# A hybrid decoder layer on one core: the first scaling and the sums of the output product stand in another order, six remainders of the mLSTM values are made by accumulating transfers, and the gates' first row waits for a sum

## The chip, the core and the metric

The kernel runs on one core of a Trainium2 chip. The metric is the device time of one execution in microseconds; the times shown are three executions of the kernel before, and one more execution was profiled. The engines are named as in the profile: PE (matrix products), DVE (vector), ACT (scalar), POOL (GpSimd) and SP (which only issues transfers here).

## What is computed

One layer of a decoder on 512 tokens with 1024 channels, in float32. The parts that the change touches:

```python
h = rmsnorm(x, norm_mix_g)                     # first scaling
proj = h @ w_in                                # mLSTM q, k, v, output gate; attention q, k, v; gates
lf = log_sigmoid(gates[..., ML_HEADS:])        # the gates' rows: lf, its sums, the running maximum
h_ml = mlstm_chunkwise(q_ml, k_ml, v_ml, ig, lf)
...
merged = sigmoid(g_a) * (y_a @ w_branch_a) + sigmoid(g_b) * (y_b @ w_branch_b)
x = x + merged @ w_out                         # output product
x = x + square(relu(rmsnorm(x, norm_mlp_g) @ w_up)) @ w_down
x = x + sigmoid(rmsnorm(x, norm_ple_g) @ w_ple_gate) * (p @ w_ple_proj)
return rmsnorm(x, final_norm_g)
```

## The kernel before

**Products in two parts.** Every float32 operand of a product is split into a high part (a rounding copy) and a low part (the remainder `value - high`), and three products high·high, high·low, low·high are summed in PSUM (`pairs`, `chain`). The high part of a weight is mostly an ACT cast (`wh`, L137), the low part a DVE subtraction (`wl`, L138). `split_by_transfer` (L144 to L148) makes the remainder in another way: ACT writes the high part (L146), ACT writes the negated value into the low tile (L147), and a transfer that POOL issues adds the value to it in memory (L148).

**Stages around the change.** The program first multiplies the per-layer embedding `p` by its weight (`early`: high parts `eh` on ACT and POOL at L303 and L305, remainders on DVE at L306), norms the four token tiles of `x` (`norm`: ACT squares and a root, DVE reciprocal and scaling, L341), turns them by PE transposes (`columns`, L354) and splits the result into `h` (ACT L359, DVE L360). The early products' PSUM is copied out (`pe`, L385 to L394) before the attention values (`vs`) take its bank. Then come the attention keys and the first queries, the mLSTM values (`w_vml`), the output gate (`w_o`), the branch gates (`w_gb`, `w_ga`), attention mixed with the other projections, mLSTM, the merge, the output product and the MLP.

**Seven products instead of eight.** `seven` computes a product of two-by-two blocks with seven block products in PSUM groups X, Y, Z. After the first block product (p1, `A11`) ACT copies X out (L570), and the second (`A12`) adds to X, so PE waits for that copy. t21 and t22 are sums that DVE makes from Z (L573); c11, c22, c12, c21 are the results. `by_tokens` runs it for `w_vml` and then for `w_o`; the sums and differences of weight blocks are DVE operations of 128x1024 (L510, L511, L520, L524). For the values, `put_v` adds the kept part on DVE (L597), casts the high part on ACT (L598), subtracts on DVE for the low part (L599) and stores the low part to memory by a POOL transfer (L584). The output product (`out_proj`, from L1108) does the same by hand: its first product is F11, then ACT copies X to `q1` (L1144), and F12 adds to X; `b11 + b12` is L1151, `b21 - b11` is L1160, `b22 - b11` is L1161.

**What sets the order.** A scheduler sorts the instructions of each engine when the program is built, by its own estimate of when each is ready; each engine then works its list strictly in order. `tc.issue_after(x)` lays an edge: the instructions in its block on x's engine come behind x. Tiles come from pools with a fixed number of buffers: weights `wr` 4, `wh` 4, `wl` 4, scratch `lm` 4, activations `act` 34. A transfer into a buffer waits until its last reader is done.

Of the kernel before, what the change touches and what calls it, by code (L numbers as in the profile page):

```python
# [13 lines left out]
ALU = mybir.AluOpType  # L14
# [22 lines left out]
def block_kernel(  # L37
# [30 lines left out]
    V, A, G, T = nc.vector, nc.scalar, nc.gpsimd, nc.tensor  # L68
# [43 lines left out]
    def act_hl(n="s"):  # L112
        return [act_r(n), act_r(n)]
# [15 lines left out]
    def r32(t):  # L129
        return t.bitcast(F32)  # L130
# [13 lines left out]
    def split_by_transfer(dst, src):  # L144

        A.copy(dst[0], src)  # L146
        A.activation(dst[1], src, AF.Copy, scale=-1.0)  # L147
        return nc.gpsimd.dma_start(out=r32(dst[1]), in_=src, accum_op=ALU.add)  # L148
# [146 lines left out]
    spare = ps_a()  # L295
    early_ps = [spare[:, :512], spare[:, 512:], ps_g(), ps_g()]

    def early_part(k):
        parts = []
        for i, t in enumerate(early[k]):  # L300
            hl = act_hl("eh")
            if k or i:
                G.tensor_copy(hl[0], t)  # L303
            else:
                p_high = A.copy(hl[0], t)  # L305
            V.tensor_sub(hl[1], t, r32(hl[0]))  # L306
            parts.append(hl)
        return parts, p_high if k == 0 else None

    def early_products(k, parts):  # L310
        for m in range(NT):
            chain(early_ps[m], pairs([q[:, m * P : (m + 1) * P] for q in parts[0]], parts[1]), k == 0, k == 1, True)

    e0, p_high = early_part(0)
    e1, _ = early_part(1)
    early_products(0, e0)

    rooted = [None]
# [48 lines left out]
    def load_vs_w(c):  # L367
        n = K3[c].stop - K3[c].start
        hl = [wp.tile([P, 1024], F32R, tag=t, bufs=WB, name=nm(t))[:, : n * 264] for t in ("wh", "wl")]
        w_high = G.tensor_copy(hl[0], wv[c][:, : n * 264])  # L370
        last_low[0] = V.tensor_sub(hl[1], wv[c][:, : n * 264], r32(hl[0]))
        return [q.rearrange("p (k c) -> p k c", k=n) for q in hl]

    with tc.issue_after(p_high.ins):
        xn, normed = norm(0)
    with tc.issue_after(normed):
        wv[0] = load_vs_w(0)
    xn1, normed = norm(1)
    with tc.issue_after(normed):
# [15 lines left out]
    on_scalar, on_vector = columns(1, xn1)  # L395
    for m in range(NT):
        if m == 1:
            columns(2, xn2)
        elif m == 2:
            with tc.issue_after(on_scalar):  # L400
                xn, _ = norm(3)
            _, on_vector = columns(3, xn)

        ps = ps_g()
        for c in range(3):
            mm_tok(ps[:, :264], wv[c], hT[K3[c]], m, first=c == 0, last=c == 2)
        t = sp.tile([P, 256], F32, tag="vs", bufs=4, name=nm("vs"))
        A.copy(t, ps[:, :256])
        gate_in = V.tensor_add(gt[:, m, :], ps[:, 256:264], bif)
        vs.append(t)  # L410
# [3 lines left out]
        mm_T(ps, load_w(wd[i], KT * P, KT), hT)  # L414
        return ps

    with tc.issue_after(on_vector):
        wk0 = load_w(w_ksw[0], KT * P, KT)

    hf[0] = tk("hf")[:, :D].rearrange("p (k c) -> p k c", k=KT)  # L420
# [141 lines left out]
    def post_by_tokens(done):  # L562

        keep = {}

        def post(what, ps):
            for t in range(2):
                if what == "p1":
                    keep["p1", t] = act_f("p1")
                    A.copy(keep["p1", t], ps[t])  # L570
                elif what[0] == "t":
                    keep[what, t] = act_f(what)
                    V.tensor_add(keep[what, t], ps[t], keep["p1", t])  # L573
                else:
                    k = None if what == "c11" else keep["p1" if what == "c12" else "t" + what[1:], t]
                    done(t + (2 if what[1] == "1" else 0), int(what[2]) - 1, ps[t], k)

        return post

    kept = []  # L580

    def store_low():
        for o, t in kept:
            nc.gpsimd.dma_start(out=o, in_=t)  # L584
        kept.clear()

    def put_v(m, nh, ps, k):
        if k is not None:
            store_low()
        o = vm[m][:, 2 * nh : 2 * nh + 2, :DV]  # L590
        two = lambda t: t.rearrange("p (h d) -> p h d", h=2)
        low = act_r("vl")
        if k is None:
            A.copy(o, two(ps))
            V.tensor_sub(two(low), two(ps), r32(o))
        else:
            V.tensor_add(k, ps, k)  # L597
            A.copy(o, two(k))  # L598
            V.tensor_sub(two(low), two(k), r32(o))  # L599
        kept.append((vld[:, 2 * nh : 2 * nh + 2, m, :], two(r32(low))))  # L600

    pg = ps_a()
# [3 lines left out]
        T.transpose(pgf[:4, m * P : (m + 1) * P], gt[:, m, 4:], ident)  # L606
    by_tokens(w_vml, post_by_tokens(put_v), True)
    store_low()


    def row(n):
        return c1.tile([P, 512], F32, tag="row", bufs=NH, name=nm(n))
# [25 lines left out]
    def gates():  # L638

        lf = row("lf")[:4, :]  # L640
        V.scalar_tensor_tensor(lf, fg, -1.0, fg, ALU.mult, ALU.max)
        A.activation(lf, lf, AF.Exp, scale=-1.0)
        A.activation(lf, lf, AF.Ln, bias=1.0)
        V.scalar_tensor_tensor(lf, fg, 0.0, lf, ALU.min, ALU.subtract)
        mst = act_f("mst")[:4, :]
        V.tensor_tensor_scan(mst, lf, ig, 0.0, ALU.add, ALU.max)
        fl = row("fl")[:4, :]
        for c in range(NT):
            V.tensor_tensor_scan(fl[:, c * P : (c + 1) * P], lf[:, c * P : (c + 1) * P], zeros4, 0.0, ALU.add, ALU.add)
# [415 lines left out]
    for j in range(4):  # L1065
        m0 = merge(2 * j)
        if j == 0:
            load_out(1)
            load_out(3)
        elif j < 3:  # L1070
            b = b_out[1][j - 1]
            V.tensor_sub(b, b_out[3][j - 1], b)
        else:
            for m in range(NT):
                nc.sync.dma_start(out=xk[m], in_=x[m * P : (m + 1) * P, :])
        later = merge_sums(m0, merge(2 * j + 1))
        if j < 3:
            later()

# [33 lines left out]
    def out_proj():  # L1113

        b11, b12, b21, b22 = b_out
        X = [ps_g(), ps_g()]
        Y, Z = [[t[:, 0, :], t[:, 1, :]] for t in (pair(), pair())]

        def form(raw):
            return load_w(None, 1024, 2, raw)  # L1120

        def half(ps, f, w, kh, first, last):
            for t in range(2):
                ops = []
                for k in range(2):
                    ops += pairs([h[:, t * P : (t + 1) * P] for h in f[2 * kh + k]], [h[:, k, :] for h in w])
                chain(ps[t], ops, first and kh == 0, last and kh == 1, True)

        def prod(ps, f, b, first, last):
            for kh in range(2):  # L1130
                half(ps, f, form(b[kh]), kh, first, last)

        def part_of(r, c, t):
            return xk[t + (2 if r == 1 else 0)][:, (c - 1) * 512 : c * 512]

        def acc(ps, r, c):
            for t in range(2):
                o = part_of(r, c, t)
                V.tensor_add(o, ps[t], o)

        prod(X, F11, b11, True, False)
        q1 = [act_f("q1") for _ in range(2)]
        for t in range(2):
            copied = A.copy(q1[t], X[t])  # L1144
        with tc.issue_after(copied.ins):
            later()
        for r, c in ((2, 1), (2, 2), (1, 2)):
            for t in range(2):
                nc.gpsimd.dma_start(out=part_of(r, c, t), in_=q1[t], accum_op=ALU.add)
        for kh in range(2):  # L1150
            V.tensor_add(b11[kh], b12[kh], b11[kh])  # L1151
        prod(X, F12, b21, False, True)
        acc(X, 1, 1)
        with tc.issue_after(last_mm[0].ins):
            prod(Z, G2, b11, True, False)
        acc(Z, 2, 1)
# [12 lines left out]
        half(Z, G4, form(b22[1]), 1, False, True)  # L1169
        acc(Z, 1, 2)  # L1170
# [386 lines left out]
```

## Time and profile before

| what | value |
|---|---|
| three runs | 877.5, 878.6, 879.84 us (median 878.6) |
| profiled execution, its own time | 877.63 us |
| its span, first to last instruction | 875.5 us |
| mean granted PE clock | 0.999 |
| busy PE / DVE / ACT / POOL | 862.2 / 674.4 / 488.9 / 51.4 us |

The profiled execution's own time is 2.1 us above its span; the rest lies before the first and behind the last instruction. Times in the rows below count from the start of the span. A row of the timeline gives start, duration, engine, line, operation, tiles, shape and count, and in brackets the idle time of the engine before it with what ended it. A duration of PE is that of a pipelined matmul; the distance of two starts is what one costs. The same holds on DVE and ACT, where the next operation starts about 0.08 us before the one ahead of it ends.

### The profile page before, as it was taken

The page shows a single profiled execution, that of the slowest core. Times are in us where ns is not written, and L with a number is a line of the kernel's source. Part 1 is how long each engine was busy: PE and PEld are TensorE (multiplying, and loading weights), DVE is VectorE, ACT ScalarE, POOL GpSimd, SP SyncE. Part 2 cuts the span into 40 slices and gives each one's busy share as a digit, 9 for nine tenths or more (in the row PEclk, how much of TensorE's full clock was granted, in tenths as well). Part 3 has the DMA queues.
Part 4 walks back from the last instruction along what each step waited for, and adds up shares of the span by engine and source line. Part 5 has one row for each costly group of instructions (what it writes and reads, how often), then busy time and mean ns, then how long its engine had stood idle before and what let it go on. Part 6 is the DMA issues. An engine that isn't in the chain of part 4 may idle for free.

```text
span 875.5 us, 11759 instructions
## 1 busy us (share of the span) xinstructions
PE 862.2 (98%) x4422; PEld 725.2 (83%) x4422; DVE 674.4 (77%) x998; ACT 488.9 (56%) x825; POOL 51.4 (6%) x81
## 2 busy tenths in 40 slices
PE   9999999999999999999999999999999999999996
PEld 7878789999877778888878888888888888888886
DVE  7899979785688898867897668756975795678657
ACT  6785556444586667853343566345535633564743
POOL 3221111000000000000020000000000000002000
PEclk9999999999999999999999999999999999999999
DMA  8686236445121255665334710531162044206502
GB/s 285 212 204 254 107 109 204 146 144 197 69 73 49 96 185 194 211 252 183 107 53 137 249 66 25 205 119 38 62 224 100 1 142 171 73 24 133 180 1 97
DMA packets 36234, 117.76 MB, mean 135 GB/s; under 512 B 5069, under 2 KB 5069, under 8 KB 36178
## 3 DMA queue, kind: packets, MB, share of 16 engines
q1 hardware_dynamic: 28578, 95.77, 31.2%
q0 software_dynamic: 7456, 20.98, 8.8%
q8 instruction: 35, 0.57, 0.3%
q10 hardware_dynamic: 144, 0.26, 0.1%
q14 instruction: 21, 0.17, 0.1%
HBM read 99.17 MB, written 11.54 MB: 126 GB/s over the span
## 4 chain that ended last, share of the span: by engine, by line
PE 87%; DVE 6%; ACT 3%; DMA 2%; issue 2%; SPq 0%; ACTq 0%; DVEq 0%
PE psg L176 48%; PE psp L176 23%; PE psa L176 6%; PE pst L176 2%; PE pst L836 2%; DVE wl L138 1%; PE psp L1105 1%; DMA wq<-in_w_o 1%; PE psa L778 1%; DMA xt<-in_x 1%; PE psa L779 1%; ACT wh L137 1%; PE psa L918 1%; PE psa L940 1%; PE psa L938 1%
## 5 line engine op out<-in xcount | busy, mean ns | idle before, releaser
L137 ACT CAST wh<-wr 128x1024 fp32r<-128x1024 f32 x129 | 135.6, 1053 | 156.4 <-PE psg L176 62.7
L138 DVE TENSOR_TENSOR wl<-wr,wh 128x1024 fp32r<-128x1024 f32 x129 | 156.8, 1219 | 74.2 <-ACT wh L137 73.1
L176 PE MATMUL psg<-x,wh 128*128 128x512 f32 x512 | 157.8, 389 | 0.0
L176 PE MATMUL psp<-wh,uf 128*128 128x512 f32 x448 | 138.6, 389 | 0.0
L176 PEld LDWEIGHTS psg<-x,wh 128*128 128x128 f32 x512 | 96.1, 188 | 19.9
L176 PE MATMUL psg<-x,wl 128*128 128x512 f32 x256 | 99.6, 389 | 0.0
L176 PEld LDWEIGHTS psp<-wh,uf 128*128 128x128 f32 x448 | 84.1, 188 | 17.5
L176 PE MATMUL psp<-wl,uf 128*128 128x512 f32 x224 | 87.2, 389 | 0.0
L176 PE MATMUL psg<-h,wh 128*128 128x512 f32 x256 | 80.9, 395 | 0.7 <-DVE rc L804 0.7
L137 ACT CAST wh<-wd 128x1024 fp32r<-128x1024 f32 x44 | 46.2, 1053 | 54.3 <-PE psp L176 21.9
L138 DVE TENSOR_TENSOR wl<-wd,wh 128x1024 fp32r<-128x1024 f32 x44 | 53.1, 1218 | 14.7 <-ACT wh L137 14.5
L176 PEld LDWEIGHTS psg<-x,wl 128*128 128x128 f32 x256 | 48.1, 188 | 9.9
L176 PEld LDWEIGHTS psg<-h,wh 128*128 128x128 f32 x256 | 46.9, 188 | 11.2 <-issue 1.6
L176 PE MATMUL psg<-h,wl 128*128 128x512 f32 x128 | 50.5, 395 | 0.0
L138 DVE TENSOR_TENSOR uf<-F,uf 128x1792 fp32r<-128x1792 f32 (+2 forms) x20 | 33.0, 1652 | 21.8 <-ACT uf L137 21.8
L176 PEld LDWEIGHTS psp<-wl,uf 128*128 128x128 f32 x224 | 42.1, 188 | 8.7
L176 PE MATMUL psg<-yb,wh 128*128 128x512 f32 x128 | 40.4, 393 | 0.0
L1273 DVE SCALAR_TENSOR_TENSOR xk<-psp,r,xk 128x512 f32<-128x512 f32 x48 | 33.8, 745 | 8.0 <-PE psp L176 7.7
L176 PE MATMUL psg<-ya,wh 128*128 128x512 f32 x128 | 39.8, 391 | 0.0
L137 ACT CAST uf<-F 128x1792 fp32r<-128x1792 f32 (+2 forms) x20 | 27.9, 1396 | 20.5 <-DVE F L1249 20.4
L176 PE MATMUL psa<-h,wh 128*128 128x256 f32 x192 | 35.5, 285 | 0.6 <-ACT p L714 0.5
L176 PE MATMUL psg<-hS,wh 128*128 128x256 f32 x192 | 35.7, 285 | 0.2 <-DVE t L704 0.2
(356 smaller groups left out, 1836.1 us busy)
## 6 DMA issues: line engine op xcount, KB each, us to landing
wr<-in_w_up SPq DMA_DIRECT2D x32, 512.0 KB, 3.2
wd<-in_w_down SPq DMA_DIRECT2D x24, 512.0 KB, 3.8
wr<-in_w_qsw SPq DMA_DIRECT2D x8, 512.0 KB, 4.3
gd<-gr POOLq DMA_DIRECT2D x8, 512.0 KB, 3.1
wr<-in_w_qkml SPq DMA_DIRECT2D x8, 512.0 KB, 3.2
wr<-in_w_b SPq DMA_DIRECT2D x8, 512.0 KB, 3.2
wh<-in_w_b POOLq DMA_DIRECT2D x8, 512.0 KB, 3.8
gl<-gd SPq DMA_DIRECT2D x8, 512.0 KB, 3.3
```

Of the source, the lines that this page charges most:

```text
L137: A.copy(dst[0], src)
L138: last_low[0] = V.tensor_sub(dst[1], src, r32(dst[0]))
L176: last_mm[0] = T.matmul(ps, l, r, start=first and i == 0, stop=last and i == len(ops) - 1, skip_group_check=parts)
L778: T.matmul(o, q[:, n * P : (n + 1) * P], kk[kp][ab][:, k0 : k0 + 256], start=True, stop=False)
L779: T.matmul(o, q[:, n * P : (n + 1) * P], kl[kp][ab][:, k0 : k0 + 256], start=False, stop=True)
L836: T.matmul(o[HALF[ab], :], v[:, c : c + 64], w[:, ab * 512 : (ab + 1) * 512], start=j == 0, stop=j == len(terms) - 1)
L918: T.matmul(psc[s], l, r, start=j == 0, stop=j == 2, skip_group_check=True)
L938: T.matmul(o, hi, vm[s][:, h, :], start=s == 0, stop=False, skip_group_check=True)
L940: last_mm[0] = T.matmul(o, lo, vm[s][:, h, :], start=False, stop=s == t, skip_group_check=True)
L1105: T.transpose(ps[:, c, m * P : (m + 1) * P], xk[m][:, (k + c) * P : (k + c + 1) * P], ident)
L1273: V.scalar_tensor_tensor(o, ps[:, t, :], r2[:, 2 * toks + t : 2 * toks + t + 1], o, ALU.mult, ALU.add)
```

## The change

Four edits. First, the early remainders are made in two separate steps: those of the first half stand where they stood, those of the second half (`early_low(1, e1)`) behind the first scaling; the norm of the last token tile moves ahead of `columns(2)`, and `columns(2)` behind it. Second, the three values results that need a sum (c22, c12, c21, two tiles each) get their low part by `split_by_transfer` in place of the DVE subtraction, and their stores lag by two. Third, the gates' first row operation (DVE) is laid behind the last t22 sum that is recorded in `summed`. Fourth, `b11 + b12` of the output product is laid behind the remainder of the last merge.

```diff
-    def early_part(k):
-        parts = []
-        for i, t in enumerate(early[k]):
-            hl = act_hl("eh")
-            if k or i:
-                G.tensor_copy(hl[0], t)
-            else:
-                p_high = A.copy(hl[0], t)
-            V.tensor_sub(hl[1], t, r32(hl[0]))
-            parts.append(hl)
-        return parts, p_high if k == 0 else None
+    def early_high(k):
+        parts = [act_hl("eh"), act_hl("eh")]
+        for hl, t in zip(parts, early[k]):
+            done = (G.tensor_copy if k or hl is parts[1] else A.copy)(hl[0], t)
...
+    def early_low(k, parts):
+        for hl, t in zip(parts, early[k]):
             V.tensor_sub(hl[1], t, r32(hl[0]))
...
-    e0, p_high = early_part(0)
-    e1, _ = early_part(1)
+    e0, p_high = early_high(0)
+    e1, _ = early_high(1)
+    early_low(0, e0)
     early_products(0, e0)
...
     with tc.issue_after(normed):
+        early_low(1, e1)
         wv[0] = load_vs_w(0)
...
         if m == 1:
-            columns(2, xn2)
+            with tc.issue_after(on_scalar):
+                xn, normed = norm(3)
+            with tc.issue_after(normed):
+                turned_third, _ = columns(2, xn2)
         elif m == 2:
-            with tc.issue_after(on_scalar):
-                xn, _ = norm(3)
             _, on_vector = columns(3, xn)
...
-                    V.tensor_add(keep[what, t], ps[t], keep["p1", t])
+                    summed[0] = V.tensor_add(keep[what, t], ps[t], keep["p1", t])
...
-    def store_low():
-        for o, t in kept:
+    def store_low(last=0):
+        while len(kept) > last:
+            o, t = kept.pop(0)
             nc.gpsimd.dma_start(out=o, in_=t)
-        kept.clear()
...
-            store_low()
+            store_low(2)
...
             V.tensor_add(k, ps, k)
-            A.copy(o, two(k))
-            V.tensor_sub(two(low), two(k), r32(o))
+            split_by_transfer([o, two(low)], two(k))
...
+    values_sum = summed[0]
...
-        V.scalar_tensor_tensor(lf, fg, -1.0, fg, ALU.mult, ALU.max)
+        with tc.issue_after(values_sum.ins):
+            V.scalar_tensor_tensor(lf, fg, -1.0, fg, ALU.mult, ALU.max)
...
-        later = merge_sums(m0, merge(2 * j + 1))
+        m1 = merge(2 * j + 1)
+        merged = last_low[0]
+        later = merge_sums(m0, m1)
...
-        for kh in range(2):
-            V.tensor_add(b11[kh], b12[kh], b11[kh])
+        with tc.issue_after(merged.ins):
+            for kh in range(2):
+                V.tensor_add(b11[kh], b12[kh], b11[kh])
```

Because the scheduler sorts anew, more moves than the diff shows. Three places follow. Lines of the changed kernel lie up to six higher.

**DVE at the start.** `eh_28`/`eh_30` and their partners are the early remainders of the second half, `xn_33` the first token tile, `wl_38` the low part of the first piece of the attention values' weight. Before:

```order
L306 TENSOR_TENSOR eh_28_177<-p_7_111,eh_27_176 128x512
L306 TENSOR_TENSOR eh_30_181<-wp_8_112,eh_29_180 128x512
L326 RECIPROCAL rs_36_204<-sd_35_202 128x1
L341 SCALAR_TENSOR_TENSOR xn_33_199<-xt_1_102,rs_36_204,psa_15_146 128x512 x2
L326 RECIPROCAL rs_42_217<-sd_41_215 128x1
L371 TENSOR_TENSOR wl_38_209<-wr_10_122,wh_37_208 128x792
```

And now:

```order
L327 RECIPROCAL rs_36_202<-sd_35_200 128x1
L342 SCALAR_TENSOR_TENSOR xn_33_197<-xt_1_102,rs_36_202,psa_15_146 128x512 x2
L308 TENSOR_TENSOR eh_28_175<-p_7_111,eh_27_174 128x512
L308 TENSOR_TENSOR eh_30_177<-wp_8_112,eh_29_176 128x512
L372 TENSOR_TENSOR wl_38_209<-wr_10_122,wh_37_208 128x792
L327 RECIPROCAL rs_42_217<-sd_41_215 128x1
```

The first scaling passed the two remainders, which now stand directly ahead of `wl_38`.

**DVE from the values' second half into the output gate's product.** `wq_182`/`wq_183` are sums of `w_o` blocks, `wl_173`/`wl_175` the low parts of the values' last product, `t22`, `p1`, `t21` the values' results c22, c12, c21, `wl_200` the low part that the output gate's second product reads. Before:

```order
L138 TENSOR_TENSOR wl_173_895<-wr_117_616,wh_172_894 128x1024
L510 TENSOR_TENSOR wq_182_946<-wq_186_954,wq_182_946 128x1024
L597 TENSOR_TENSOR t22_158_805<-psa_121_624,t22_158_805 128x512
L597 TENSOR_TENSOR t22_159_807<-psa_121_624,t22_159_807 128x512
L138 TENSOR_TENSOR wl_175_911<-wr_118_618,wh_174_910 128x1024
L599 TENSOR_TENSOR vl_164_843<-t22_158_805,vm_108_590 128x512
L599 TENSOR_TENSOR vl_165_848<-t22_159_807,vm_109_592 128x512
L597 TENSOR_TENSOR p1_130_661<-psg_124_627,p1_130_661 128x512
L138 TENSOR_TENSOR wl_194_964<-wr_180_942,wh_193_963 128x1024
```

And now, from the sum on:

```order
L513 TENSOR_TENSOR wq_182_952<-wq_186_960,wq_182_952 128x1024
L600 TENSOR_TENSOR t22_158_805<-psa_121_624,t22_158_805 128x512
L600 TENSOR_TENSOR t22_159_807<-psa_121_624,t22_159_807 128x512
L138 TENSOR_TENSOR wl_173_897<-wr_117_616,wh_172_896 128x1024
L138 TENSOR_TENSOR wl_175_913<-wr_118_618,wh_174_912 128x1024
L513 TENSOR_TENSOR wq_183_954<-wq_187_962,wq_183_954 128x1024
L600 TENSOR_TENSOR p1_130_661<-psg_124_627,p1_130_661 128x512
L138 TENSOR_TENSOR wl_194_970<-wr_180_948,wh_193_969 128x1024
L600 TENSOR_TENSOR p1_131_663<-psg_125_628,p1_131_663 128x512
L138 TENSOR_TENSOR wl_196_986<-wr_181_950,wh_195_985 128x1024
L514 TENSOR_TENSOR wr_180_948<-wq_182_952,wr_180_948 128x1024
L514 TENSOR_TENSOR wr_181_950<-wq_183_954,wr_181_950 128x1024
```

The remainders (L599) are gone, but `wl_173` now stands behind the sum, and the second sums stand further ahead. The next three rows are `wl_200` and the two sums of c21; before, `wl_200` stood behind c21 and its remainders.

**ACT at the first product of `w_o`, and at the output product.** `wh_205` is a cast for the third product, `p1_197` the copy of X. Before, and now:

```order
L598 CAST vm_108_590<-t21_152_769 128x2x256
L598 CAST vm_109_592<-t21_153_771 128x2x256
L137 CAST wh_205_1042<-wr_180_942 128x1024
L570 COPY p1_197_995<-pst_189_959 128x512
L570 COPY p1_198_997<-pst_190_960 128x512
```

```order
L146 CAST vm_108_590<-t21_152_769 128x2x256
L147 ACTIVATE vl_176_929<-t21_152_769 128x512
L146 CAST vm_109_592<-t21_153_771 128x2x256
L147 ACTIVATE vl_177_935<-t21_153_771 128x512
L137 CAST wh_205_1048<-wr_180_948 128x1024
L573 COPY p1_197_1001<-pst_189_965 128x512
L573 COPY p1_198_1003<-pst_190_966 128x512
```

Two more passes stand ahead of the copy. In the output product the cast `wh_853` of `b11` after its sum stands ahead of the copy of X, `q1_845`, in both; but its sum (L1157 now) has moved on DVE behind the last merge:

```order
L137 CAST mg_825_4593<-sga_824_4590 128x512
L137 CAST ms_829_4603<-ms_827_4597 128x512
L137 CAST wh_853_4707<-wr_831_4607 128x1024
L1149 COPY q1_845_4657<-psg_837_4621 128x512
L1149 COPY q1_846_4658<-psg_838_4622 128x512
```

What moved there is the moment at which the cast's input is ready.

More of the change, by code (lines that the diff above doesn't have):

```diff
@@ L296, in block_kernel @@
     early_ps = [spare[:, :512], spare[:, 512:], ps_g(), ps_g()]
-    def early_part(k):
-        parts = []
-        for i, t in enumerate(early[k]):
-            hl = act_hl("eh")
-            if k or i:
-                G.tensor_copy(hl[0], t)
-            else:
-                p_high = A.copy(hl[0], t)
+    def early_high(k):
+        parts = [act_hl("eh"), act_hl("eh")]
+        for hl, t in zip(parts, early[k]):
+            done = (G.tensor_copy if k or hl is parts[1] else A.copy)(hl[0], t)
+            if not k and hl is parts[0]:
+                first = done
+        return parts, first if k == 0 else None
+    def early_low(k, parts):
+        for hl, t in zip(parts, early[k]):
             V.tensor_sub(hl[1], t, r32(hl[0]))
-            parts.append(hl)
-        return parts, p_high if k == 0 else None
     def early_products(k, parts):
@@ L415, in proj_T @@
         return ps
-    with tc.issue_after(on_vector):
+    with tc.issue_after(on_vector), tc.issue_after(turned_third):
         wk0 = load_w(w_ksw[0], KT * P, KT)
```

## The prediction

> **What bounds the kernel now.** I read the page first.
>
> ```profile
> span 875.5 us, 11759 instructions
> PE 862.2 (98%) x4422; PEld 725.2 (83%) x4422; DVE 674.4 (77%) x998; ACT 488.9 (56%) x825; POOL 51.4 (6%) x81
> PE 87%; DVE 6%; ACT 3%; DMA 2%; issue 2%; SPq 0%; ACTq 0%; DVEq 0%
> ```
>
> PE is busy for 862.2 of 875.5 us and makes 87% of the chain that ended last. The change takes no matmul away and adds none. So it acts only through moments at which PE stands still, and each of its four edits must be costed at the PE wait beside it. The list of PE's waits came second.
>
> ```profile
> PE pst L176 <- DVE wl L138: 0.9, 1, 0.9
> PE psg L176 <- DVE sga L1020: 0.9, 1, 0.9
> PE pst L354 <- ACT sd L324: 0.7, 1, 0.7
> ```
>
> Columns: total, times, longest. The first wait lies in the output gate's product, the second at the merge, the third at the first transposes. All three lie beside an edit, and together they are 2.5 us: what four edits could win is about this large. Third I read the timeline around the three places.
>
> **The first scaling.** Four engines, in order of time:
>
> ```profile
> 8.94 0.29 ACT L324 ACTIVATE sd<-ss,eps_t 128x1 f32<-128x1 f32 x1
> 8.97 0.61 POOL L303 CAST eh<-wp 128x512 fp32r<-128x512 f32 x1
> 9.00 1.12 DVE L306 TENSOR_TENSOR eh<-p,eh 128x512 fp32r<-128x512 f32 x1 [2.15 <-POOL eh L303]
> 10.04 0.68 DVE L306 TENSOR_TENSOR eh<-wp,eh 128x512 fp32r<-128x512 f32 x1
> 10.90 1.41 DVE L341 SCALAR_TENSOR_TENSOR xn<-xt,rs,psa 128x512 f32<-128x512 f32 x2
> 11.26 0.85 POOL L370 CAST wh<-wr 128x792 fp32r<-128x792 f32 x1 [1.68 <-DMA wr<-in_w_vsif]
> 11.79 1.22 PE L354 MATMUL pst<-ident,xn 128*128 128x128 f32 x8 [0.66 <-ACT sd L324]
> 12.25 1.72 POOL L370 CAST wh<-wr 128x792 fp32r<-128x792 f32 x1
> 12.29 0.96 DVE L371 TENSOR_TENSOR wl<-wr,wh 128x792 fp32r<-128x792 f32 x1
> 15.69 0.68 DVE L388 COPY pe<-psg 128x512 f32<-128x512 f32 x1
> 16.52 0.36 PE L176 MATMUL psg<-wh,h 128*128 128x264 f32 x1
> ```
>
> The root `sd` ends at 9.23. In the new order DVE then takes the reciprocal and the two scalings (1.41 and its overlap: about 9.5 to 10.8), and only then the two remainders, 0.60 and 0.68, to 12.1. The transposes can therefore start near 10.9 instead of 11.79. That gain is spent at once, because PE's next need is the values' product at 16.52, and what leads there is DVE's list: low parts of the weight, scaling of the next tile, remainders of `h`, the copy `pe` at 15.69. DVE does the same work as before, so this list moves only if DVE waits somewhere. It does: the cast of the first weight piece on POOL arrives at 11.26, tied to its transfer. Before, it ran beside the scaling and took 0.85; the same cast at 12.25, beside a DVE subtraction with two operands in SBUF, took 1.72. The remainder at 9.00 took 1.12 beside the POOL cast at 8.97, against 0.68 at 10.04 without one. So a POOL cast and such a subtraction go one after the other. In the new order the cast at 11.26 meets the two remainders: they end at 12.1, the cast needs its 0.85 after that and ends near 12.96, and `wl`, which reads it, starts at 13.0 instead of 12.29: +0.7. At best POOL slips in ahead of both and `wl` starts when DVE is free, at 12.13: −0.2. At worst POOL's second cast follows at once and shuts `wl` out too, which costs its 0.85 more (the cast alone, row 11.26): +1.55. I take **+0.7**, the reading that both rows with a collision share.
>
> The Trainium skill (SBUF — State Buffer, section "SBUF: two separate sides") says of this that a VectorE operation with two SBUF inputs and a GpSimd operation that reads SBUF take one shared pair of ports, and whichever starts first keeps it for the whole instruction. The rows 1.72 beside 0.85 agree; by the rule the cast could also win the pair between the two remainders, and `wl` would still come at 13.0, since the second remainder would then run last.
>
> **From the values to the output gate.** The remainders by transfer (L598 to L600 in the changed kernel) take six DVE subtractions away, 0.60 each by their pitch, and put six ACT passes and six POOL transfers in their place. The rows that carry the path:
>
> ```profile
> 56.64 0.61 ACT L146 CAST hS<-s 128x512 fp32r<-128x512 f32 x1
> 57.15 0.63 ACT L147 ACTIVATE hS<-s 128x512 fp32r<-128x512 f32 x1
> 63.40 0.39 PE L176 MATMUL psg<-wh,hS 128*128 128x512 f32 x1
> 64.07 0.47 PE L176 MATMUL psg<-wh,hS 128*128 128x512 f32 x1 [0.28 <-DVE t L573]
> 73.68 1.19 DVE L138 TENSOR_TENSOR wl<-wr,wh 128x1024 fp32r<-128x1024 f32 x1
> 76.47 1.23 DVE L510 TENSOR_TENSOR wq<-wq,wq 128x1024 f32<-128x1024 f32 x1 [1.60 <-DMA wq<-in_w_o]
> 77.61 1.28 DVE L597 TENSOR_TENSOR t<-psa,t 128x512 f32<-128x512 f32 x2
> 88.09 1.28 DVE L597 TENSOR_TENSOR t<-psa,t 128x512 f32<-128x512 f32 x2
> 88.80 1.22 ACT L598 CAST vm<-t 128x512 fp32r<-128x512 f32 x2 [1.59 <-DVE t L597]
> 89.93 1.05 ACT L137 CAST wh<-wr 128x1024 fp32r<-128x1024 f32 x1
> 90.88 0.57 ACT L570 COPY p<-pst 128x512 f32<-128x512 f32 x1
> 91.62 2.35 DVE L138 TENSOR_TENSOR wl<-wr,wh 128x1024 fp32r<-128x1024 f32 x2
> 92.89 0.50 PE L176 MATMUL pst<-wl,h 128*128 128x512 f32 x1 [0.88 <-DVE wl L138]
> ```
>
> Before, the second product's first matmul could run at about 91.5, when the copy ended (90.88 + 0.57); PE was done with the first product then. Its second matmul had to wait for the low part `wl_200` until 92.89: with the copy and the low part together PE stood some 1.3 still. In the new order `wl_200` is no longer late, since it stands ahead of c21. But another chain takes its place. At 76.47 DVE waits for the transfer of `w_o`. The low part at 73.68 and the gates' first rows used to stand ahead of this wait and were done in its time; now they stand behind it, so DVE idles for about 4 us (the 1.60 and some 2.5 of these operations), and the wait still ends at 76.47, as the transfer is what it was. From there DVE's list holds, up to the sums of c21, nine operations of 1024 columns at 1.14 (76.47 to 77.61) and four of 512 at 0.60 (two take 1.28 less the overlap of about 0.08): 10.3 + 2.4 = 12.7. So c21 starts at 89.1, where it started at 88.09. ACT begins 0.71 behind it (88.80), at 89.8, with four passes instead of two, 0.51 each (56.64 to 57.15): 91.85; the cast `wh_205`, 0.95 (89.93 to 90.88): 92.8; the copy of X, 0.57: 93.4. The second product starts at 93.5. Before, that product ran without a break from one spacing (0.23) ahead of 92.89, as if begun at 92.65: +0.85. Against this stands one matmul that PE's new order puts into the wait at 63.40 to 64.07, ahead of the sums it waits for: −0.23. The four other transfers' passes lie on ACT where it is idle (1.59 ahead of 88.80), and the transfers themselves end at memory well ahead of mLSTM. Together **+0.6**; at best the whole wait is gone, −1.3 − 0.23 = −1.5; the upper end is the third rival's.
>
> **The output product.** Again in order of time:
>
> ```profile
> 445.68 0.69 DVE L1020 TENSOR_TENSOR sga<-psg,gl 128x512 f32<-128x512 f32 x1 [0.37 <-PE psg L176]
> 447.22 1.22 DVE L138 TENSOR_TENSOR wl<-wr,wh 128x1024 fp32r<-128x1024 f32 x1
> 449.58 1.06 ACT L137 CAST wh<-wr 128x1024 fp32r<-128x1024 f32 x1 [1.57 <-PE psg L176]
> 449.63 0.42 DVE L1040 TENSOR_TENSOR ms<-ms,sga 128x256 f32<-128x256 f32 x1
> 451.06 0.57 ACT L1144 COPY q<-psg 128x512 f32<-128x512 f32 x1
> 451.82 0.61 PE L176 MATMUL psg<-wh,mg 128*128 128x512 f32 x2
> ```
>
> Taking `b11 + b12` off the path ahead of the merge doesn't shorten the merge's wait: the row at 445.68 waits for PE itself, so 0.88 stays. Behind the merge DVE now runs product, sum and low part of the merge (446.28, 446.88 with 1.14, 448.0 with 0.60), three operations of 256 columns at 0.34 (the last at 449.63 before), and then `b11 + b12`, from 449.6 to 450.85. The cast `wh_853` starts at 450.9 instead of 449.58, and in ACT's list it stands ahead of the copy of X: 450.9 + 0.95 = 451.85, and 0.57 for the copy: 452.4. PE wants that copy at 452.05, the second matmul of the last row. Before, the copy ended at 451.63 and nobody waited. **+0.45**, between 0 (the operations of 256 columns fall behind) and +0.8 (one more pass of ACT, `ms`, ahead).
>
> The gates' first row (third edit) is off PE's path: the rows' results are needed only at mLSTM, far behind, so I cost it at nothing beyond the move past the wait at 76.47, which is counted above.
>
> **Sum.** 0.7 + 0.6 + 0.45 = +1.75 us on the profiled execution's 877.63, so 879.4. The median of three stands 0.97 above that execution: **880.35, given as 880.4**. A measurement of this kernel can tell about 0.3% from no change, which is 2.6 us, from 876.0 to 881.2.
>
> **Rivals.**
>
> *The covers come through (faster, below the bound of what can be told or beyond it).* POOL slips in first (−0.2), the transfer of `w_o` lands 2 us earlier (93.5 less 91.5) because fewer small transfers stand ahead of it, so that the copy is not late and the wait of 1.3 goes (−1.5), and the cast is on time (0): −1.7, 876.9. It speaks for it that `wl_200` really moves ahead. Against it: the row at 76.47 shows the landing as a wait of 1.60 already. It passes 876.0 only if one more of the waits, such as the 0.66 at the first transposes, is won too.
>
> *Both casts shut DVE out.* POOL's second cast follows its first with no gap, so the low part waits for it as well: +1.55 instead of +0.7, so +2.6 and 881.2 in all, at the very bound of what can be told. For it: the row at 9.00 is such a collision. Against it: `wl` at 12.29 started 0.04 behind a cast and made that cast wait, not the other way.
>
> *The last weight transfers come late (slower).* `wl_173` and `wl_175` now read their weight buffers last at 80.0 and 81.1 (76.47 + 1.14 + 1.20, and 1.14 more for each), where the first was free at 74.87 before. The buffers take the last two blocks of `w_o`, and their transfers then run beside four of the accumulating transfers.
>
> ```profile
> wr<-in_w_o SPq DMA_DIRECT2D x4, 512.0 KB, 4.2
> wq<-in_w_o SPq DMA_DIRECT2D x4, 512.0 KB, 6.9
> hS<-s POOLq DMA_DIRECT2D x8, 256.0 KB, 4.2
> ```
>
> The last column is the median from issue to landing. At 4.2 they land at 84.2 and 85.3, and nothing waits. In the list above `wl_200` is due at 89.1 less its 1.14, at 88.0, and its cast takes 0.95 before; so it decides from 7.0 us on (landing at 87.0), and from there each microsecond is one of PE's, since the sums of c21, ACT's passes and the copy of X all stand behind it. At 8.4, twice the median of the same tile, it is +1.4 on top of 1.75: 881.75. For it: the 6.9 of the second row, where four transfers of this size overlap. Against it: only two overlap here, and the first row is the same tile.
>
> **Chances.** The forecast 0.50; covers come through 0.20; both casts 0.15; late transfers 0.15. That the change does nothing of what it says is not open, since the lists of the engines show it. The range takes in the first rival, 876.8, and above the third with the upper end of the output product (+0.35) and half of the second's difference (+0.85): 882.5. Faster by over 0.3%: somewhat under half of the first rival, 0.09. Slower by over 0.3%: most of the third (0.12), half of the second (0.07) and the forecast's upper edge (0.05): 0.24. The rest, 0.67, lies within.
>
> **What would show it.** In the changed kernel's profile: transposes near 10.9; a POOL cast of about 1.7 from 11.3 and `wl` at 13.0; the first matmul of the values' product near 17.2. DVE's wait for `wq<-in_w_o` grown from 1.6 to about 4, ending at 76.5. PE waiting for ACT `p` (L573) at the output gate's product until 93.5, in place of DVE `wl`, and a new wait of PE for ACT `q` (L1149) of about 0.45. The prediction is wrong if that matmul starts at 16.5 or earlier, if the second product of the output gate starts at 92.7 or earlier, or if `q` is not waited for.

## The result, and the profile after

The changed kernel takes 883.05 us (median of five runs, 882.63 to 884.65); the kernel before has a median of 878.53 over five. The ratio is 1.0059, with a 95% interval of 1.0048 to 1.0071: slower, by about 4.5 us, where 880.4 was forecast and 882.5 was the upper end. The profiled execution took 882.63 us, its span is 880.9. First the page and PE's waits of the changed kernel.

```profile
span 880.9 us, 11772 instructions
PE 864.4 (98%) x4422; PEld 727.1 (83%) x4422; DVE 671.8 (76%) x992; ACT 492.0 (56%) x831; POOL 56.5 (6%) x87
```

```profile
PE pst L176 <- ACT p L573: 3.2, 1, 3.2
PE psg L176 <- DVE pe L390: 1.1, 1, 1.1
...
PE psg L176 <- DVE sga L1023: 0.9, 1, 0.9
...
PE psg L176 <- ACT q L1149: 0.4, 1, 0.4
```

The same number of matmuls, as expected. The wait for `wl` is gone and one for the copy of X (`p`) has taken its place, as the forecast said; but it is 3.2 us long, not about 1. The wait for `q` is there with the forecast 0.4. Matching the matmuls of the two traces one by one (both have 4422) shows where the loss arises: the changed kernel is later by 0.9 us behind the start (at 22 us), still by 0.9 just ahead of the wait for `p`, by 3.0 at its end, by 4.7 four microseconds further on, and by 5.4 from the output product to the end. The stretch in the middle, in order of time, on four engines:

```profile
76.36 1.23 DVE L513 TENSOR_TENSOR wq<-wq,wq 128x1024 f32<-128x1024 f32 x1 [3.13 <-DMA wq<-in_w_o]
78.75 0.63 ACT L147 ACTIVATE vl<-t 128x512 fp32r<-128x512 f32 x1
79.69 1.89 POOL L148 DMA_DIRECT2D vl<-t  x2 [16.68 <-ACT vl L147]
79.95 1.46 SPq L186 DMA_DIRECT2D wr<-in_w_o  x2
82.83 0.62 ACT L146 CAST vm<-p 128x512 fp32r<-128x512 f32 x1 [0.17 <-DVE p L600]
86.04 0.63 ACT L147 ACTIVATE vl<-p 128x512 fp32r<-128x512 f32 x1 [2.59 <-DMA vl<-t]
88.57 0.63 ACT L147 ACTIVATE vl<-p 128x512 fp32r<-128x512 f32 x1 [1.38 <-DMA vl<-t]
89.10 1.99 ACT L137 CAST wh<-wr 128x1024 fp32r<-128x1024 f32 x2
90.17 1.23 DVE L138 TENSOR_TENSOR wl<-wr,wh 128x1024 fp32r<-128x1024 f32 x1 [2.23 <-ACT wh L137]
91.31 1.28 DVE L600 TENSOR_TENSOR t<-psa,t 128x512 f32<-128x512 f32 x2
92.03 0.62 ACT L146 CAST vm<-t 128x512 fp32r<-128x512 f32 x1 [0.94 <-DVE t L600]
94.13 1.03 ACT L137 CAST wh<-wr 128x1024 fp32r<-128x1024 f32 x1
95.06 1.06 ACT L573 COPY p<-pst 128x512 f32<-128x512 f32 x2
95.69 0.50 PE L176 MATMUL pst<-wh,h 128*128 128x512 f32 x1 [3.25 <-ACT p L573]
```

DVE's wait for `w_o` ends at 76.36, where the forecast had it. What the forecast did not have is on ACT: the negations at 86.04 and 88.57 do not wait for their operand, but for the accumulating transfers of c22 (`vl<-t`). Their output tiles come from the pool of 34 activation buffers, and so the two buffers that are handed to them must be the ones of the tiles `t22`, which those transfers still read; the first two experiments test this. ACT works in order, so the two casts of `w_o` behind (89.10), the low part `wl_200` on DVE (90.17), the sums of c21 (91.31), ACT's four passes, the cast and the copy of X all slide by some 2 us. The issue list tells how long such a transfer takes (last column, median from issue to landing, us):

```profile
hS<-s POOLq DMA_DIRECT2D x8, 256.0 KB, 4.0
...
vl<-t POOLq DMA_DIRECT2D x4, 256.0 KB, 6.3
...
vl<-p POOLq DMA_DIRECT2D x2, 256.0 KB, 3.7
```

The windows show the rest (columns: busy time of PE, PEld, DVE, ACT and POOL, then granted PE clock, DMA share, GB/s):

```profile
92.00:93.00 1.00, 0.44 (x2) 0.02 (x1) 1.00 (x2) 0.97 (x2) 0.00 (x0) 1.00 1.04 186
93.00:95.00 2.00, 0.00 (x0) 0.00 (x0) 2.00 (x3) 2.00 (x4) 0.98 (x2) 1.00 0.69 160
95.00:97.00 2.00, 1.31 (x6) 1.07 (x7) 2.00 (x2) 2.00 (x4) 2.00 (x3) 1.00 0.51 203
97.00:100.00 3.00, 3.00 (x9) 2.33 (x8) 3.00 (x5) 0.07 (x1) 0.92 (x2) 0.50 0.97 174
```

PE resumes at 95.69, and from 97 to 100 its granted clock is 0.50. These three microseconds of half speed are the step from 3.0 to 4.7.

### The profile page after: what moved, and what is told of

Same layout as the page of the kernel before. It is cut to its first block, busy times and chain, and to the rows that moved or that the text cites. A ratio compares the mean times of both kernels' runs of the same rounds, so it can differ in the third digit from the quotient of the medians.

```text
span 880.9 us, 11772 instructions
## 1 busy us (share of the span) xinstructions
PE 864.4 (98%) x4422; PEld 727.1 (83%) x4422; DVE 671.8 (76%) x992; ACT 492.0 (56%) x831; POOL 56.5 (6%) x87
## 4 chain that ended last, share of the span: by engine, by line
PE 68%; issue 3%; DVE 3%; ACT 2%; DMA 0%; POOL 0%; POOLq 0%; ACTq 0%
PE psg L176 39%; PE psp L176 23%; PE pst L839 1%; PE psa L176 1%; PE psp L1110 1%; ACT lm L804 1%; PE psa L781 1%; PE psa L782 1%; PE psa L818 0%; DMA wh<-in_w_b 0%; DVE qs L490 0%; ACT wh L137 0%; PE pst L981 0%; DVE wl L138 0%; PE psa L921 0%
```

## The experiments

All times are medians of five to eleven runs, beside 878.5 to 878.8 for the kernel before (16 to 27 runs beside them).

**The low tiles elsewhere.** One pair of low tiles is taken from another pool (`pT`), which no engine works on here. The edit moves the tiles of c22, where the expectation says c12; since the pool hands buffers out in turn, c12's then get the ones that c22's had, which is what was wanted.

```diff
-        low = act_r("vl")
+        if k is not None and m < 2 and nh == 1:
+            if m == 0:
+                spare_low[0] = sp.tile([P, 1024], F32R, tag="pT", bufs=2, name=nm("vl"))
+            low = spare_low[0][:, m * 512 : (m + 1) * 512]
+        else:
+            low = act_r("vl")
```

> The changed kernel, with the low tiles of c12 (the two that wait) taken from an idle tile of another pool instead of from the 34 activation buffers; nothing else. Theory (buffer): ACT's negations at 86.0 and 88.6 wait only because their buffers are still read by the accumulating transfers of c22; with other buffers ACT goes on at 83.4, the casts of w_o start near 85, PE's wait for the copy of X falls from 3.25 us to about 1.1, and the granted clock stays at 1.0 afterwards: about 3.2 us less than the changed kernel, 2.1 above the kernel before (880.6). Rival (passes): the twelve ACT passes and the reordered DVE list alone make the wait; it stays near 3 us and the time at 883. Rival (transfers): the late weight transfers hold the casts up anyway; the wait stays above 2.5 us.

It took 880.3 us, ratio 1.002 (1.0011 to 1.0029): 2.7 us of the loss gone. ACT no longer waits at the negations. One row of its timeline shows where the same wait went:

```profile
91.92 0.57 ACT L573 COPY p<-pst 128x512 f32<-128x512 f32 x1
94.94 0.59 ACT L573 COPY p<-pst 128x512 f32<-128x512 f32 x1 [2.45 <-DMA vl<-p]
```

The first copy of X is 3.1 us earlier than in the changed kernel; the second now gets a buffer that the accumulating transfer of c12 still reads, and PE waits 1.4 us for it. So the wait moves with the buffer, and neither the passes nor the weight transfers make it.

**No shared buffers.** The same, with the pairs of both c22 and c12 elsewhere (condition `nh == 1` without `m < 2`).

> The changed kernel, with the low tiles of c22 and of c12 in an idle tile pair of another pool, so that neither ACT's negations nor the copies of X for w_o take a buffer that an accumulating transfer still reads. Theory (buffers): against the run in which one pair was moved, the wait of 1.4 us of PE for the second copy of X goes too; PE waits at most 0.6 us at the output gate's second product, and what is left above the kernel before is the output product's 0.7: 879.2 (878.8 to 879.8). Rival (passes): ACT's passes and the cast ahead of the copy hold X by themselves, PE waits 1 us or more and the time stays at 880.3. Rival (late weight transfers): PE waits for a low part of w_o instead, 880.5 or more.

878.09 us, ratio 0.9998 (0.9989 to 1.0007): the whole loss is gone, within what can be told, although every instruction of the four edits is still there. DVE, ACT and PE at the place:

```profile
75.26 1.22 DVE L513 TENSOR_TENSOR wq<-wq,wq 128x1024 f32<-128x1024 f32 x1 [2.80 <-DMA wq<-in_w_o]
...
82.30 0.63 ACT L147 ACTIVATE vl<-p 128x512 fp32r<-128x512 f32 x1
...
83.98 0.63 ACT L147 ACTIVATE vl<-p 128x512 fp32r<-128x512 f32 x1
...
92.26 0.50 PE L176 MATMUL pst<-wh,h 128*128 128x512 f32 x1 [0.59 <-ACT p L573]
```

No wait for a transfer on ACT, and 0.59 for the copy. The theory of the buffers holds for the wait. But not all of the 3.4 us by which the second product now begins earlier (92.26 after 95.69) is the buffers': DVE's wait for `w_o` already ends 1.1 earlier (75.26 after 76.36). From that wait to the second product it is 19.3 us in the changed kernel and 17.0 here, so the shared buffers are 2.3 of the 3.4. The other 1.1 goes with a side effect of the edit, for the pool was not idle: two weight blocks of `w_gb` are loaded into it. In the changed kernel these two transfers leave ahead of those of `w_o`, and here behind them, once the low tiles are stored (first the changed kernel, then this one):

```profile
60.82 3.22 SPq L186 DMA_DIRECT2D wq<-in_w_gb  x2
```

```profile
90.33 8.26 SPq L186 DMA_DIRECT2D wq<-in_w_gb  x2
```

In the three kernels that use this pool, the transfer of `w_o` that DVE waits for lands at 75.1 to 75.9; in the nine others that were traced, at 76.0 to 77.1. No run moves these loads alone, so how much of the time they give back was not separated. As an estimate, the passes alone make a wait of 0.9 in the changed kernel (17.0 behind 76.36 is 93.4, and PE is done with the first product at 92.44), no more than the 0.9 that the low part cost before.

**The second edit alone.** Kernel before, with the transfers only.

```diff
-            store_low()
+            store_low(2)
...
-            A.copy(o, two(k))
-            V.tensor_sub(two(low), two(k), r32(o))
+            split_by_transfer([o, two(low)], two(k))
```

> The kernel before with the second edit alone (six remainders by accumulating transfers); the gates' row stays where it was, so the low part ahead of DVE's wait for w_o stays ahead of it, and the weight transfer into its buffer leaves at about 75 instead of 80. Theory (the two edits work on each other): only one weight transfer runs beside the accumulating ones, these land in about 4 us instead of 5.4 to 6.9, ACT waits at most 1 us for buffers, PE's wait is 1 to 2 us, no halved clock: between -0.3 and +0.8 us against before. Rival (buffers alone): the transfers land as late without the gates' edit, and it costs the whole 3.8 us: 882.4.

882.51 us, ratio 1.0036 (1.0024 to 1.0049). My expectation, that the gates' edit was needed for the damage, fell: the wait is there without it. ACT waits once, for 3.32, in place of 2.59 and 1.38:

```profile
86.46 0.63 ACT L147 ACTIVATE vl<-p 128x512 fp32r<-128x512 f32 x1 [3.32 <-DMA vl<-t]
```

```profile
92.00:96.00 4.00, 0.25 (x3) 0.02 (x1) 4.00 (x5) 3.67 (x7) 2.63 (x4) 1.00 0.59 180
96.00:100.00 4.00, 4.00 (x18) 3.31 (x19) 3.93 (x5) 2.29 (x3) 1.51 (x2) 1.00 0.78 176
```

PE stands 3.75 us here, and in this execution the clock behind the wait stays at 1.00. It took 880.29; of the other four, one took 880.83 at a mean clock of 0.997, and three took 882.5 to 882.9 at 0.993 to 0.995. So the longer times, some 2 us apart, go with a lower mean clock. Where the clock fell in them is not on record; by an estimate, one stretch of half speed as in the changed kernel lowers the mean by 0.002 (half of 3.4 us in 880), and these lost more than that.

**PE kept busy during the wait.** Idle matmuls between the first and the second product of the output gate, into a bank of PSUM not yet in use.

```diff
+        def fill():
+            with tc.issue_after(last_mm[0].ins):
+                for i in range(24):
+                    done = T.matmul(Z[0][:, :P], ones, ones, start=True, stop=True)
+                    tc.keep_in_program_order(done)
+            return done.ins
```

> The changed kernel with 24 idle matmuls of 128 columns (2.6 us) put on PE between the first and the second product of the output gate, into a PSUM bank not yet in use; they fill most of PE's wait of 3.25 us and add nothing to the result. Theory (clock): the wait stays as long, but PE isn't idle, so the granted clock isn't halved behind it: 1.6 us less than the changed kernel, 881.4, and the spread of the runs shrinks (no runs at 884). Rival (the clock falls for another reason, or the slow matmuls are an effect of the transfers beside them): 883 as before, spread as before. Rival: the idle matmuls themselves delay PE, 883.5 or more.

883.83 us, ratio 1.006 (1.0048 to 1.0073), inconclusive as a price: these float32 matmuls came as 48 records and took 5.5 us, so that the second product began at 96.9. With 12 of them:

> The changed kernel with 12 idle float32 matmuls in place of 24 between the first and the second product of the output gate: the 24 gave 48 records and 5.5 us, ran past the end of the wait and delayed the second product from 95.7 to 96.9; 12 give 2.8 us and end inside the wait. Theory (clock): no halved clock behind the wait, and PE not delayed: 881.4 to 882.0, no run at 884. Rival (the slow matmuls behind the wait have another reason): the clock falls behind it all the same, 883 and runs up to 884.6.

883.51 us, ratio 1.0056 (1.0044 to 1.0069): no gain in time, against my expectation. The trace shows where the gain stood and where it went.

```profile
92.00 2.84 PE L568 MATMUL psg<-ones 128*128 128x128 f32 x24
95.63 0.50 PE L176 MATMUL pst<-wh,h 128*128 128x512 f32 x1 [0.80 <-ACT p L582]
...
147.24 0.51 PE L176 MATMUL psg<-hS,wh 128*128 128x256 f32 x2 [1.26 <-DVE t L716]
```

```profile
92.00:96.00 4.00, 3.21 (x27) 2.97 (x26) 4.00 (x5) 4.00 (x8) 2.02 (x3) 1.00 0.67 157
96.00:100.00 4.00, 4.00 (x19) 3.30 (x18) 4.00 (x5) 2.09 (x4) 1.30 (x2) 1.00 0.91 200
```

The second product begins at 95.63, as in the changed kernel, and the clock stays at 1.00. At 101 us this kernel is 1.7 us ahead of the changed one, and at 140 still 1.4. At 147 no more than 0.25 is left: PE waits 1.26 us for a DVE sum of the branch gate. POOL, ACT and DVE there, first in this kernel and then in the changed one:

```profile
140.69 0.54 POOL L666 DMA_DIRECT2D rrd<-rr  x1 [6.95 <-DVE gg L670]
144.81 1.28 ACT L674 ACT_TABLE_LOAD   x1 [2.30 <-DMA rrd<-rr]
146.77 0.76 DVE L716 TENSOR_TENSOR t<-psg,p 128x256 f32<-128x256 f32 x2 [1.36 <-ACT em L674]
```

```profile
142.07 0.54 POOL L657 DMA_DIRECT2D rrd<-rr  x1 [6.95 <-DVE gg L661]
145.07 1.28 ACT L665 ACT_TABLE_LOAD   x1 [1.18 <-DMA rrd<-rr]
147.03 0.76 DVE L707 TENSOR_TENSOR t<-psg,p 128x256 f32<-128x256 f32 x2 [0.25 <-ACT em L665]
```

The sum stands on DVE behind the wait for `em`, and `em` on ACT behind the gates' row's way through memory (`rrd`). That row was not late by itself: its transfer left 1.4 us earlier than in the changed kernel (140.69 after 142.07), as far ahead as PE. But it landed after 4.1 us instead of 2.9. In ten of the twelve kernels traced it took 2.6 to 3.3, and 3.7 in the one with 24 idle matmuls; why it is longer in these two stays open. So this trace does not tell what the slow matmuls cost in the end: what the kept clock had won was lost again to one slow transfer. That PE kept at work keeps its clock is likely, not shown by one trace, since the clock stayed up without idle matmuls too in the second edit alone; the mean clocks speak for it, 0.996 to 0.999 in the eleven runs with idle matmuls (median 0.998) and 0.995 to 0.997 in the five of the changed kernel (median 0.996). The runs at 884 us and over are there in this kernel too (885.29 at a mean clock of 0.996, 884.18 at 0.999), so the halved clock doesn't explain them; what does stays open.

**The start alone**, the first edit as in the diff of the change.

> The kernel before with the first edit alone (order at the start). Theory: the collision of POOL's casts with DVE's remainders and low parts, read off the changed kernel's trace, costs 0.75 us by itself and nothing gives it back: 879.3. Rival: PE makes it up at a later wait that is set by transfers, and the time is that of before within 0.2 us. Rival (the early transposes help): 0.3 us or more below before.

878.28 us, ratio 0.9998 (0.9989 to 1.0007): nothing. **The output product alone**, the fourth edit:

> The kernel before with the fourth edit alone (the sum b11 + b12 behind the last merge). Theory: the late cast ahead of the copy of X costs what the changed kernel's trace shows there, 0.75 us: 879.3. Rival: 0.45 us as the wait alone (the rest of the shift came with other edits). Rival: nothing, since the last phases of the kernel absorb it.

879.2 us, ratio 1.0007 (0.9998 to 1.0016). These two traces answer for the start together; PE's first matmul of the values' product, with the first edit and then, in the run of the fourth edit, with the order of before:

```profile
17.42 0.36 PE L176 MATMUL psg<-wh,h 128*128 128x264 f32 x1 [0.98 <-DVE pe L390]
```

```profile
12.46 1.63 DVE L371 TENSOR_TENSOR wl<-wr,wh 128x792 fp32r<-128x792 f32 x1
17.35 0.36 PE L176 MATMUL psg<-wh,h 128*128 128x264 f32 x1 [0.53 <-DVE pe L388]
```

The old order comes to 17.35 as well; `wl` met a POOL cast there too, and took 1.63 instead of 0.96. The 16.52 of the profile before was an early execution, not the order's time: over all traces this matmul starts at 16.5 to 17.5 in the six kernels with the old order and at 16.7 to 17.9 in the six with the new one. And a delay at the start is mostly absorbed: with the first edit alone PE is 0.8 behind the profile before at 22 us and 0.15 at 93, since DVE's wait for `w_o` ends at nearly the same moment in both (76.62 and 76.47).

For the output product, the cast of `b11 + b12` was then moved behind the copies:

```diff
-            prod(Z, G2, b11, True, False)
+            with tc.issue_after(copied.ins):
+                prod(Z, G2, b11, True, False)
```

> The kernel before with the fourth edit, and the cast of b11 + b12 moved on ACT behind the two copies of X in the output product. Theory: the 0.74 us that the fourth edit alone costs in its trace is that cast standing ahead of the copy; with the copy first, PE's wait for q of 0.44 and the step of 0.74 at 453 us are gone, 878.5, and nothing new waits since the third product needs the cast only some 5 us later. Rival: the late sum itself delays the low part and the next sums on DVE, and 0.3 us or more stay.

878.33 us, ratio 0.9996 (0.9987 to 1.0005). The step of 0.74 us at 453 in the trace of the fourth edit alone is gone, and the copies wait for PE instead of PE for them:

```profile
453.69 0.50 PE L176 MATMUL psg<-wh,mg 128*128 128x512 f32 x1 [0.44 <-ACT q L1146]
```

```profile
452.14 0.59 ACT L1146 COPY q<-psg 128x512 f32<-128x512 f32 x1 [0.39 <-PE psg L176]
453.50 0.59 ACT L1146 COPY q<-psg 128x512 f32<-128x512 f32 x1 [0.77 <-PE psg L176]
```

The first line is of the fourth edit alone, the other two with the copy first. Both intervals of the times hold 1, so this term rests on the traces.

**A better version.** In the kernel before, the two passes of c21 were moved behind the copies of X, once without transfers and once with them and without shared buffers.

```diff
-                    A.copy(keep["p1", t], ps[t])
+                    copied = A.copy(keep["p1", t], ps[t])
+                    if t == 1 and put_off:
+                        with tc.issue_after(copied.ins):
+                            while put_off:
+                                put_off.pop(0)()
+                        store_low()
```

> The kernel before, with nothing but the cast and the subtraction of c21 moved behind the copies of X for w_o (no accumulating transfers). Theory: the low part that PE waited for in the kernel before comes 1.2 us earlier, and the wait of 0.9 for it goes: 877.7 (877.3 to 878.2). Rival: DVE's list from its wait for w_o on is what counts and leaves the low part late: 878.5, no change.

877.94 us, ratio 0.9994 (0.9985 to 1.0003): no difference that can be told. In its trace PE is 1.1 us ahead at 93 and has lost it at 104, in two new waits for DVE's and ACT's work of the next products:

```profile
103.18 0.49 PE L176 MATMUL psa<-wh,hS 128*128 128x512 f32 x1 [0.40 <-ACT wh L137]
104.09 0.50 PE L176 MATMUL psg<-wh,hS 128*128 128x512 f32 x1 [0.42 <-DVE t L578]
```

> The kernel before with the second edit alone (remainders by transfer), the low tiles of c22 and c12 in the idle pair of tiles, and the two passes of c21 behind the copies of X for w_o. Theory: with no shared buffers and no passes ahead of the copy, PE's wait at the output gate's second product falls from 1.3 us in before to 0.3 or less: 877.6 (877.2 to 878.1), faster than both. Rival (contention): the accumulating transfers delay the weight transfers of w_o and DVE with them, so that the low part comes late: 878.5 or more.

877.2 us, ratio 0.9983 (0.9974 to 0.9992): faster than both kernels. Here PE does not wait between 90 and 106; of the window around the two waits 1.97 of 2 us are busy:

```profile
102.00:104.00 2.00, 1.97 (x10) 1.31 (x8) 2.00 (x4) 0.49 (x1) 1.92 (x3) 1.00 0.86 184
```

So transfers in place of the subtractions come to 1.5 us below the kernel before (by the medians), once they hold no buffer that ACT needs and their passes do not stand ahead of a copy that PE waits for. The loads of `w_gb` have moved behind those of `w_o` in this kernel as well; what that alone is worth was not tested.

## Why the prediction was wrong

**The step that failed** is the sentence that the four other transfers' passes lie on ACT where it is idle and "the transfers themselves end at memory well ahead of mLSTM". Who reads the result was checked there, not who needs the source's buffer. The tiles `t22` go back to a full pool, and the next in line for them are ACT's own negations. With 4.2 us, the median of the old transfers, the first would have landed at 83.9 (79.69 + 4.2), half a microsecond behind the moment at which ACT was free for the negation (82.83 and a pass of 0.53); it took until 86, and the second until 88.5. Price: PE is later by 3.0 us at the end of the wait (the 0.9 of the start does not add to it, since the chain starts from DVE's wait for `w_o`, which ends at 76.36, and at 76.47 in the kernel before). Of these, 2.3 are the buffers' and 0.8 the longer chain of passes that was forecast (17.0 us behind that wait, where the kernel before took 16.2, up to 92.65), less the 0.1 by which that wait ends earlier. Another 1.6 come behind it, at the half clock, which the forecast did not have. In all that is 4.7, against 0.6 forecast for the whole place.

**The chain ahead of the copy of X** was right in its order, names and starting point (76.36; the copy with its four passes and a cast ahead), and in size: forecast was a second product 17.0 us behind the end of DVE's wait (93.5 less 76.47), and with no shared buffers it is 17.0 (92.26 less 75.26). That this kernel stands level with the one before all the same goes with `w_o`, which landed 1.1 us earlier there; how much of it that explains was not tested.

**The third rival** named the right neighbours, weight transfers and accumulating ones beside each other, and the wrong victim: it let the weights come late. The two transfers `wr<-in_w_o` took 4.7 and 6.3 us, longer than the 4.2 it started from, and landed at 84.7 and 87.3, ahead of the casts at 89.10, which waited for ACT's list; the accumulating transfers were the ones that came too late. Its 881.75 came nearest, by another way.

**The start**, +0.7: wrong in kind. The collision is there, but in the order before as well, and what it costs is mostly absorbed at the next wait that a transfer sets. The early transposes did not come either: the scaling ended near 10.7, but PE, busy with the early products, began them at 11.75, where 10.9 was forecast. The profile before was an early execution at this place. The Trainium skill's rule of the shared ports (SBUF — State Buffer, "SBUF: two separate sides") agrees with the 1.63 here as with the 1.72, in that the two operations go one after the other; it just does not tell the two orders apart. Its other half, that the one that starts first goes first, the rows do not bear out: the cast of 1.72 began 0.04 ahead of `wl` (12.25 and 12.29) and was the one that waited.

**The output product**, +0.45: mechanism right, shown by moving the cast; in the trace the step is 0.74 us, of which the wait for `q` is 0.44. The gates' edit was costed at nothing, and nothing here speaks against that: the second edit alone, without it, is only 0.5 us below the whole change, about what the fourth edit costs by itself (879.2 against 878.5). The third edit had no run of its own.

None of the prediction's three signs of being wrong came: the matmul started at 17.51, the second product at 95.69, and `q` was waited for. All three asked whether the effects were smaller than forecast, and the one that failed was larger.

**The base**: the sum was made against a profile 0.97 below the median, and the shift by 0.97 was right.

## What to carry to other kernels

A transfer that replaces an engine's operation keeps its source and its target occupied until it lands. Ask, for each tile of the source, which instruction gets its buffer next, and on which in-order queue that instruction stands. Terms ahead of a wait that a transfer sets don't add to terms behind it. One profiled execution has its own luck at the start, and a run of an edit elsewhere shows what of a shift that is. An edit made to test one cause can move transfers far away: before its time is put down to that cause, look whether the waits ahead of the place still end where they did.

## What the runs showed of the hardware

In the changed kernel the six accumulating transfers of 256 KB took, from issue to landing, 6.3 and 7.8 us (c22), 3.3 and 4.1 (c12), 3.6 and 6.4 (c21). The two of c22 ran beside weight transfers of 512 KB that left at 80 and 81; that these made them long was not tested by a run of its own, and with one such transfer beside them, in the second edit alone, those of c22 took 5.9 and 6.1 and ACT still waited 3.32 us.

The gates' row, 8 KB to memory, took 2.6 to 4.1 us to land in the twelve kernels traced.

After a wait of 3.25 us PE's granted clock was 0.50 for over three microseconds in one execution; after one of 3.75 us it stayed at 1.00 in another. The Trainium skill (TensorE: Matmul & The Clock Gate, section "Part 1: The HAM clock gate (the "warmup" mystery)") has PE's clock fall to half after at least one idle window of about 3.4 us, and says that this window runs freely. Taken strictly, 3.25 us are too short for a whole window, and the clock fell all the same (the 3.25 count from the end of the last matmul, which the profile only models, so the gap to 3.4 is not a sure one); that it did not after 3.75 us fits a window whose start is not tied to the idle stretch. With PE kept busy over most of the wait it stayed at 1.00 in the two traces with idle matmuls.
